# Tiles that TensorE reads moved to multiples of 512 bytes in a decoder layer

## The chip, the cores and the metric

The kernel runs on one core of one Trainium2 chip. The metric is the device time of one execution in microseconds (us); the median of three runs stands for the kernel. The engines are named as in the profile: PE is TensorE (its weight loads are listed apart as PEld), DVE is VectorE, ACT is ScalarE, POOL is GpSimd, SP is SyncE, which here issues nearly all DMAs.

## The reference

One decoder layer on 256 tokens of 2048 features in float32: two groups of 8 attention heads of 128 features each, an output projection, an MLP of 8192 hidden features with squared ReLU, and RMSNorms before, between and after.

```python
def reference(x, norm1_g, w_in, forget_b, rel_bias, outnorm_a_g, outnorm_b_g, w_out,
              norm2_g, w_mlp_in, w_mlp_out, final_norm_g):
    B, S, _ = x.shape                                   # 1, 256
    for l in range(DEPTH):                              # 1
        h = rms_norm(x, norm1_g[l])
        proj = h @ w_in[l]                              # 2048 -> 6 x 1024 + 8
        q_a, k_a, v_a, f_a, q_b, k_b, v_b = jnp.split(proj, SPLIT_POINTS, axis=-1)
        ...
        log_f = jax.nn.log_sigmoid(f_a.astype(jnp.float32) + forget_b[l].astype(jnp.float32))
        y_a = fox_attention(heads_a(q_a), heads_a(k_a), heads_a(v_a), log_f)   # causal, with a decay per key
        ...
        y_b = dilated_attention(heads_b(q_b), heads_b(k_b), heads_b(v_b), rel_bias)
        ...
        mixed = jnp.concatenate([rms_norm(y_a, outnorm_a_g[l]),
                                 rms_norm(y_b, outnorm_b_g[l])], axis=-1)
        x = x + mixed @ w_out[l]
        h = rms_norm(x, norm2_g[l])
        x = x + jnp.square(jax.nn.relu(h @ w_mlp_in[l])) @ w_mlp_out[l]
    return rms_norm(x, final_norm_g)
```

## The kernel before, in words

**Arithmetic.** Every large product is made of three: a float32 operand is split into a rounded part `hi` and the rest `lo` (both of type float32r), and hi·hi, lo·hi and hi·lo are added up in PSUM. ACT makes `hi` and DVE makes `lo`; for the weights that is `split_rows` (L168, L169), which reads the tile `raw` that a DMA has filled and writes `whi` and `wlo`.

**Chunks and steps.** The weights are cut into chunks of 512 columns: 12 chunks of q, v and k (each 16 blocks of 128 rows deep), 8 of the output projection ("o", 8 blocks), and four rounds of 4 up chunks ("u") and 4 down chunks ("d"), 16 blocks each. A step is two blocks of one chunk. The loop at the end of the kernel goes through all steps in order: it loads ahead, splits the weights up to `LEAD` = 3 steps ahead, issues the step's products, and then runs whatever was set down for that place with `at(...)` (attention, norms, drains, transposes). The order of the instructions is written out by hand, and no planner changes it.

**The products on PE.** A matmul has a stationary operand, which its own weight load (PEld) brings in first, and a moving operand, which streams through.
- q, v, k, o and d chunks (`product`, L299 to L301): stationary are 128 columns of the activations (`aT_hi`/`aT_lo` for q, v, k; `big_hi`/`big_lo` for o and d), moving are 512 columns of `whi` or `wlo`.
- u chunks (`turned_product`, L313): stationary are 128 columns of `whi` or `wlo`, moving are 256 columns of `aT_hi` or `aT_lo`.
- The last d chunk (`last_chunk`) does its second row block in two halves of 256 columns, and half of its split weights lie in `aT_hi` and `aT_lo`.
- Attention uses matmuls of 128 and 256 columns: L490 and L493 for the scores (k moving, q stationary), L538 for the values (`p_hi`/`p_lo` moving, v stationary); L520, L463 and L250 are transposes.

**Where the tiles lie.** All of SBUF's tiles come from pools (`one`, `two`, `wraw`, `wsplit`), laid out one behind the other in the order in which the pools are entered, and inside a pool in the order of first use; a tile's size is rounded up to 32 bytes. The first pool begins at byte 16512 of each partition, which is 128 past a multiple of 512. Since tiles of 8 to 2592 bytes stand among the large ones, the large ones begin at odd places. From the sizes in the code, the start of each tile modulo 512 bytes is:

| tile | role on PE | start mod 512 before |
|---|---|---|
| `xs`, `ident` | transposes | 128 |
| `aT_hi`, `aT_lo` | stationary for q, v, k; moving for u | 480 |
| `big_hi`, `big_lo` (`yT`, `hT`) | stationary for o and d | 160 |
| `whi`, `wlo` (four buffers each) | moving for q, v, k, o, d; stationary for u | 160 |
| `q_hi`, `q_lo`, `v_hi`, `v_lo` | stationary in attention | 480 |
| `k_hi`, `k_lo`, `p_hi`, `p_lo` | moving in attention | 288 |
| `gate_s`, `gate_h` | decay term of the scores | 160, 416 |
| `raw` (four buffers) | not read by PE | 160, 288, 416, 32 |

Every slice that a large product reads begins a whole number of 512 bytes behind its tile's start, so the column holds for the slices too. A float32r element has 4 bytes: a moving operand of 512 columns is 2048 bytes in a partition, one of 256 columns 1024, a stationary operand 512.

**The constant pack.** `pk` holds, for the first attention group, two triangular matrices for the decay sums, and the causal mask as three blocks of 128 columns (triangle, zeros, triangle); L503 adds the first block to the scores of the first 128 queries and the other two to those of the second.

Of the kernel before, what the change touches and what calls it, by code (L numbers as in the profile page):

```python
# [11 lines left out]
F32 = mybir.dt.float32  # L12
# [7 lines left out]
P = 128  # L20
D_MODEL = 2048
SEQ = 256
TB = SEQ // P
HD = 128
NH = 8
# [7 lines left out]
N_BUCKETS = 32  # L33
# [9 lines left out]
def _constants():  # L43
    i = np.arange(P)
    upto = (i[:, None] <= i[None, :]).astype(np.float32)
    after = (i[:, None] > i[None, :]).astype(np.float32)
    tri = np.where(i[None, :] <= i[:, None], 0.0, NEG).astype(np.float32)
    head = (i[:, None] % 32 == np.arange(NH)[None, :]).astype(np.float32)
    pack = np.concatenate([after, -upto, tri, np.zeros((P, P), np.float32), tri, head], axis=1)

    dist = np.arange(RW) - 127
    d = np.maximum(dist, 0)
    exact = N_BUCKETS // 2
    df = np.maximum(d.astype(np.float32), np.float32(1.0))
    large = exact + (
        np.log(df / np.float32(exact)) / np.float32(math.log(REL_MAX / exact)) * np.float32(N_BUCKETS - exact)
    ).astype(np.int32)
    bucket = np.where(d < exact, d, np.minimum(large, N_BUCKETS - 1))
    count = np.zeros(RW, np.int64)
    for window, dil in PATTERNS:  # L60
        count += (dist >= 0) & (dist % dil == 0) & (dist <= window)
    pick = np.zeros((N_BUCKETS + 1, RW), np.float32)
    pick[bucket, np.arange(RW)] = 1.0
    pick[N_BUCKETS] = np.where(count > 0, np.log(np.maximum(count, 1)), NEG)
    return np.ascontiguousarray(pack), pick
# [3 lines left out]
def kernel(  # L69
# [20 lines left out]
    o2d = out.rearrange("b (t p) d -> p (b t) d", p=P)  # L90
    w_in, w_out, w_up, w_down = w_in[0], w_out[0], w_mlp_in[0], w_mlp_out[0]

    one = ctx.enter_context(tc.tile_pool(name="one", bufs=1))
    two = ctx.enter_context(tc.tile_pool(name="two", bufs=2))
    wraw = ctx.enter_context(tc.tile_pool(name="wraw", bufs=4))
    wsplit = ctx.enter_context(tc.tile_pool(name="wsplit", bufs=LEAD + 1))
    psum = ctx.enter_context(tc.tile_pool(name="psum", bufs=2, space=PSUM))
    dram = ctx.enter_context(tc.tile_pool(name="dram", bufs=1, space=DRAM))
    ctx.enter_context(tc.manual_schedule())
# [74 lines left out]
    ident = one.tile([P, P], F32, name="ident")  # L174
    zeros = two.tile([P, CW], F32, name="nat")
    warm = zeros[:, :CW // 2].bitcast(BF16)
    half_t = one.tile([P, TB], F32, name="half_t")
    ones = one.tile([P, 1], F32, name="ones")
    nc.vector.memset(zeros[:, :CW // 2], 0.0)
    nc.vector.memset(half_t, -0.5)  # L180
    nc.vector.memset(ones, 1.0)
# [12 lines left out]
    for c in range(1, 4):  # L194
        load_x(4 * c, 4 * c + 4)
        load(2 * c)
    fb = one.tile([P, NH], F32, name="fb")
    relx = one.tile([N_BUCKETS + 1, NH], F32, name="relx")
    nc.vector.memset(relx, 1.0)
    pk = one.tile([P, 5 * P + NH], F32, name="pk")  # L200
    pick_sb = two.tile([P, RW], F32, name="pr")[:N_BUCKETS + 1]

    def small_loads():
# [4 lines left out]
        nc.sync.dma_start(pk, pack)  # L208
        nc.sync.dma_start(pick_sb, pick)

    mcat = pk[:, 2 * P:5 * P]
    head = pk[:, 5 * P:]
    gcat = one.tile([P, TB, P], F32R, name="gcat")


# [4 lines left out]
            nc.tensor.matmul(pw, warm[:, :P], warm, start=True, stop=True)  # L220

    nc.scalar.activation(ones, ones, AF.Copy)
    gT = one.tile([P, 48], F32, name="gT")

    def gains(k0, k1):
        p = psum.tile([P, 512], F32, name="tr")
# [28 lines left out]
    def rsqrt(dst, ssq, n):  # L255

        w = dst.shape[1]
        v = two.tile([P, TB], F32, name="rs_v")[:, :w]
        t = two.tile([P, TB], F32, name="rs_t")[:, :w]
        nc.vector.tensor_scalar(v, ssq, 1.0 / n, EPS, op0=ALU.mult, op1=ALU.add)  # L260
        nc.gpsimd.tensor_tensor(dst, v, half_t[:, :w], op=ALU.pow)
        nc.vector.tensor_tensor(t, dst, dst, op=ALU.mult)
        nc.vector.tensor_tensor(t, t, v, op=ALU.mult)
        nc.vector.tensor_scalar(t, t, -0.5, 1.5, op0=ALU.mult, op1=ALU.add)
        nc.vector.tensor_tensor(dst, dst, t, op=ALU.mult)

    ssq1 = one.tile([P, TB, 4], F32, name="ssq1")
    ssq1s = one.tile([P, TB], F32, name="ssq1s")
    rstd1 = one.tile([P, TB], F32, name="rstd1")
    rstdq = one.tile([P, TB], F32, name="rstdq")  # L270

    def first_squares(t, c):
        unused = yT_hi[:, 2 * (4 * t + c):2 * (4 * t + c) + 2, :].rearrange("p k s -> p (k s)")
# [66 lines left out]
        side.setdefault(i, []).append((f, a))  # L340


    logf = one.tile([P, TB, NH], F32, name="logf")
    lf_hi, lf_lo = (
        two.tile([P, 3 * P], F32R, name=n)[:, :2 * P].rearrange("p (t q h) -> p t q h", t=TB, q=4)
        for n in ("p_hi", "p_lo")
# [10 lines left out]
    def forget_gates():  # L357
        f = psum.tile([P, 512], F32, name="tr")
        for t in range(TB):
            nc.tensor.transpose(f[:, 2 * t * NH:2 * (t + 1) * NH], fTs[0][:, t * P:(t + 1) * P], ident[:2 * NH, :2 * NH])  # L360
        z = one.tile([P, TB, NH], F32, name="fz")
        e = one.tile([P, TB, NH], F32, name="fe")
        u = one.tile([P, TB, NH], F32, name="fu")
        d = one.tile([P, TB, NH], F32, name="fd")
        n = one.tile([P, TB, NH], F32, name="fn")
        for t in range(TB):
            for k, add in enumerate((fb, z[:, t, :])):
                nc.vector.scalar_tensor_tensor(
                    z[:, t, :], f[:, (2 * t + k) * NH:(2 * t + k + 1) * NH], rstd1[:, t:t + 1], add,
                    op0=ALU.mult, op1=ALU.add,  # L370
                )
        nc.scalar.activation(e, z, AF.Abs)
        nc.scalar.activation(e, e, AF.Exp, scale=-1.0)

        nc.vector.tensor_scalar(u, e, 1.0, None, op0=ALU.add)
        nc.vector.tensor_scalar(d, u, 1.0, None, op0=ALU.subtract)
        nc.vector.tensor_scalar(n, d, 0.0, None, op0=ALU.is_equal)
        nc.vector.tensor_tensor(d, d, n, op=ALU.add)
        nc.vector.reciprocal(d, d)
        nc.scalar.activation(u, u, AF.Ln)  # L380
        nc.vector.tensor_tensor(u, u, d, op=ALU.mult)
        nc.vector.tensor_tensor(u, u, n, op=ALU.add)
        nc.vector.tensor_tensor(u, u, e, op=ALU.mult)
        nc.vector.scalar_tensor_tensor(logf, z, 0.0, u, op0=ALU.min, op1=ALU.subtract)
        split_psum(lf_hi[..., :NH], lf_lo[..., :NH], logf[:, :, None, :].to_broadcast([P, TB, 4, NH]))
# [25 lines left out]
    relT = one.tile([P, NH, SEQ], F32, name="relT")  # L411
# [67 lines left out]
    def scores(g, h):  # L479

        half, kind = groups[g][3:]
        hd = half * 4 + h
# [14 lines left out]
        decay.pop(hd, None)  # L497
        neg = two.tile([P, 3 * P], F32, name="neg")
        pr = two.tile([P, 3 * P], F32, name="pr")
        st = two.tile([P, 3, TB], F32, name="st")  # L500
        for t, c0, c1 in spans:
            add = mcat[:, c0:c1] if kind == 0 else relT[:, hd, SEQ - (c1 - c0):]
            nc.vector.tensor_tensor_reduce(  # L503
                neg[:, c0:c1], s[:, c0:c1], add, -1.0, BIG, ALU.add, ALU.min, st[:, 0, t:t + 1]
            )
# [41 lines left out]
        split_psum(yT_hi[:, hd, :], yT_lo[:, hd, :], y[:, :SEQ], gT[:, 32 + hd:33 + hd])  # L547
        seen[kind] += 1

    rstdo = [one.tile([P, TB], F32, name=f"rstdo{k}") for k in range(2)]  # L550

    def group_norm(kind):
        p = psum.tile([P, 512], F32, name="tr")
# [2 lines left out]
                             skip_group_check=True)  # L556
        rsqrt(rstdo[kind], p[:, :TB], D_GRP)

    ssq2 = one.tile([P, TB, 4], F32, name="ssq2")
    ssq2s = one.tile([P, TB], F32, name="ssq2s")  # L560
    rstd2 = one.tile([P, TB], F32, name="rstd2")
    rstd2sq = one.tile([P, TB], F32, name="rstd2sq")

    def drain_o(kind, c, ci):
        acc = accs.pop(ci)
# [26 lines left out]
            )  # L592

    gf = relT.rearrange("p h s -> p (h s)")
    ssq3 = one.tile([P, TB, 5], F32, name="ssq3")
    ssq3s = one.tile([P, TB], F32, name="ssq3s")
    rstd3 = one.tile([P, TB], F32, name="rstd3")

    def load_gf():
        nc.sync.dma_start(  # L600
# [21 lines left out]
    def put_gain(t, cs):  # L622
        nc.vector.tensor_tensor(xs[:, t, cs], xs[:, t, cs], gf[:, cs], op=ALU.mult)
# [5 lines left out]

    def finish(t, n, cs):  # L630
        r, s = rstd3[:, t:t + 1], ssq3s[:, t:t + 1]
        v = two.tile([P, 1], F32, name="fi_v")
        u = two.tile([P, 1], F32, name="fi_u")
        ru = two.tile([P, 1], F32, name="fi_ru")
        nc.vector.tensor_scalar(v, ssq3[:, t, n:n + 1], s, 1.0 / D_MODEL, op0=ALU.add, op1=ALU.mult)
        nc.gpsimd.tensor_tensor(r, v, half_t[:, :1], op=ALU.pow)
        put_gain(t, cs)
        nc.vector.scalar_tensor_tensor(u, r, v, r, op0=ALU.mult, op1=ALU.mult)
        nc.vector.tensor_scalar(u, u, -0.5, 1.5, op0=ALU.mult, op1=ALU.add)
        nc.gpsimd.tensor_tensor(ru, r, u, op=ALU.mult)  # L640
        for c, (a, b) in enumerate(((0, 384), (384, 896), (896, 1408), (1408, 2048))):
            xc = xs[:, t, a:b]
            if c == 1:
                nc.scalar.activation(xc, xc, AF.Copy, scale=ru)
            else:
                nc.vector.tensor_scalar(xc, xc, r, u, op0=ALU.mult, op1=ALU.mult)  # L646
            nc.sync.dma_start(o2d[:, t, a:b], xc)
# [27 lines left out]
    for ci, (what, key, *_rest) in enumerate(chunks[:-1]):  # L675
        e = last_slot[what, key]
# [9 lines left out]
        elif what in "qk":  # L686
# [4 lines left out]
            if what == "k":  # L691
                kind = groups[key][4]
                for h in range(4):
                    n = e + 6 + 4 * h
# [45 lines left out]
    upto = {final - 4: final, final - 3: final + 1, final - 2: final + 3, final - 1: final + 5}  # L740
# [42 lines left out]
```

## Time and profile before

| | |
|---|---|
| median of three runs | 1136.5 us (1136.19 to 1137.27) |
| time of the profiled execution | 1136.86 us |
| its span in the profile | 1135.1 us |
| PE busy | 1124.0 us, 99% |
| PEld, DVE, ACT, POOL busy | 87%, 56%, 46%, 3% |
| DMA | 209.15 MB, mean 184 GB/s |
| mean granted PE clock | 0.998 |

Matmuls overlap in the profile: one that starts is listed with its whole way through the array, so the durations in the rows are longer than the distance between two starts. What the engine needs for one of a long row of matmuls is the distance from start to start, and it is read here as a stretch of time divided by the number of matmuls that start in it.

### The profile page before, as it was taken

The numbers are of one execution on the slowest core, as the hardware profiler recorded it, in microseconds if no ns is written. First come the engines' busy times: TensorE is split into PE (matmuls) and PEld (weight loads), VectorE is DVE, ScalarE is ACT, GpSimd is POOL, SyncE is SP. The second block draws the span as 40 slices with busy tenths as digits, with TensorE's granted clock in tenths as the row PEclk, the third lists the DMA queues.
The fourth block names the chain that finished last, engine by engine and source line by source line (L and its number), as shares of the span: only waits on it lengthen the run. The fifth ranks groups of instructions, "written<-read, shape, count | busy, mean of one in ns | idle before, by whom it ended". The sixth has DMA issues, their size and how long they took to land.

```text
span 1135.1 us, 16038 instructions
## 1 busy us (share of the span) xinstructions
PE 1124.0 (99%) x6635; PEld 988.8 (87%) x6635; DVE 639.7 (56%) x795; ACT 521.9 (46%) x675; POOL 31.7 (3%) x57
## 2 busy tenths in 40 slices
PE   9999999999999999999999999999999999999996
PEld 6778888888888889998889998889998889999886
DVE  5665656556566665555555555545555554555564
ACT  5545545545445554454334444343544433454451
POOL 0100200100001000000000000000000000000000
PEclk9999999999999999999999999999999999999999
DMA  8655454454545556556555655566465566556642
GB/s 312 224 183 183 154 185 149 149 185 149 186 156 178 155 179 192 187 179 212 196 185 164 208 186 188 200 199 192 152 220 187 186 193 192 187 171 206 240 148 74
DMA packets 104933, 209.15 MB, mean 184 GB/s; under 512 B 3651, under 2 KB 4508, under 8 KB 104732
## 3 DMA queue, kind: packets, MB, share of 16 engines
q1 hardware_dynamic: 104556, 207.06, 55.8%
q0 software_dynamic: 304, 1.06, 0.3%
q8 instruction: 52, 0.85, 0.3%
q14 instruction: 21, 0.17, 0.0%
HBM read 206.00 MB, written 2.11 MB: 183 GB/s over the span
## 4 chain that ended last, share of the span: by engine, by line
PE 98%; DMA 1%; DVE 0%; SPq 0%; ACT 0%; POOL 0%; issue 0%; DVEq 0%
PE acc L313 32%; PE acc L299 21%; PE acc L301 21%; PE acc L300 21%; PE sc L493 1%; PE sc L538 1%; PE tr L463 1%; DMA raw<-in_w_in_dram 1%; PE tr L250 1%; PE tr L520 0%; PE sc L333 0%; PE sc L490 0%; DVE wlo L169 0%; ACT whi L168 0%; DVE xs L646 0%; SPq L185 0%
## 5 line engine op out<-in xcount | busy, mean ns | idle before, releaser
L169 DVE TENSOR_TENSOR wlo<-raw,whi 128x1024 fp32r<-128x1024 f32 (+1 forms) x381 | 464.1, 1224 | 374.4 <-ACT whi L168 371.6
L168 ACT ACTIVATE whi<-raw 128x1024 fp32r<-128x1024 f32 (+1 forms) x381 | 399.8, 1055 | 404.2 <-PE acc L300 241.4
L313 PE MATMUL acc<-aT_hi,whi 128*128 128x256 f32 x1024 | 287.2, 280 | 0.0
L313 PE MATMUL acc<-aT_hi,wlo 128*128 128x256 f32 x1024 | 286.1, 279 | 0.0
L313 PE MATMUL acc<-aT_lo,whi 128*128 128x256 f32 x1024 | 286.0, 279 | 0.0
L299 PE MATMUL acc<-whi,big_hi 128*128 128x512 f32 (+1 forms) x632 | 246.0, 389 | 0.0
L301 PE MATMUL acc<-wlo,big_hi 128*128 128x512 f32 (+1 forms) x632 | 244.7, 387 | 0.0
L300 PE MATMUL acc<-whi,big_lo 128*128 128x512 f32 (+1 forms) x632 | 244.5, 387 | 0.0
L313 PEld LDWEIGHTS acc<-aT_hi,wlo 128*128 128x128 f32 x1024 | 192.8, 188 | 0.0
L313 PEld LDWEIGHTS acc<-aT_hi,whi 128*128 128x128 f32 x1024 | 192.3, 188 | 0.2
L313 PEld LDWEIGHTS acc<-aT_lo,whi 128*128 128x128 f32 x1024 | 191.6, 187 | 0.2
L299 PE MATMUL acc<-whi,aT_hi 128*128 128x512 f32 x384 | 157.0, 409 | 0.0
L300 PE MATMUL acc<-whi,aT_lo 128*128 128x512 f32 x384 | 152.5, 397 | 0.0
L301 PE MATMUL acc<-wlo,aT_hi 128*128 128x512 f32 x384 | 152.3, 397 | 0.0
L301 PEld LDWEIGHTS acc<-wlo,big_hi 128*128 128x128 f32 x632 | 118.7, 188 | 24.4
L300 PEld LDWEIGHTS acc<-whi,big_lo 128*128 128x128 f32 x632 | 118.8, 188 | 23.4
L299 PEld LDWEIGHTS acc<-whi,big_hi 128*128 128x128 f32 x632 | 118.8, 188 | 22.9
L301 PEld LDWEIGHTS acc<-wlo,aT_hi 128*128 128x128 f32 x384 | 72.5, 189 | 17.4
L299 PEld LDWEIGHTS acc<-whi,aT_hi 128*128 128x128 f32 x384 | 72.7, 189 | 15.3 <-issue 0.6
L300 PEld LDWEIGHTS acc<-whi,aT_lo 128*128 128x128 f32 x384 | 72.7, 189 | 14.0 <-DVE aT_lo L240 0.2
L237 DVE TENSOR_TENSOR big_lo<-nat,big_hi 128x512 fp32r<-128x512 f32 x32 | 22.2, 693 | 22.3 <-ACT big_hi L236 22.3
L507 ACT ACTIVATE pr<-neg,st 128x128 f32<-128x128 f32 (+1 forms) x32 | 14.3, 448 | 40.8 <-DVE st L503 40.8
(160 smaller groups left out, 533.7 us busy)
## 6 DMA issues: line engine op xcount, KB each, us to landing
raw<-in_w_mlp_in_dram SPq DMA_DIRECT2D x64, 1024.0 KB, 5.3
raw<-in_w_mlp_out_dram SPq DMA_DIRECT2D x64, 1024.0 KB, 5.2
raw<-in_w_in_dram SPq DMA_DIRECT2D x42, 1024.0 KB, 5.2
raw<-in_w_out_dram SPq DMA_DIRECT2D x16, 1024.0 KB, 5.1
raw<-in_w_in_dram SPq DMA_DIRECT2D x4, 1040.0 KB, 5.3
raw<-in_w_in_dram SPq DMA_DIRECT2D x3, 512.0 KB, 8.6
xs<-in_x_dram SPq DMA_DIRECT2D x3, 512.0 KB, 9.6
big_lo<-rel_d POOLq DMA_DIRECT2D x1, 1024.0 KB, 7.3
```

What stands on the lines that cost most here:

```text
L168: nc.scalar.activation(hi, t, AF.Copy)
L169: nc.vector.tensor_tensor(lo, t, hi.bitcast(F32), op=ALU.subtract)
L237: nc.vector.tensor_tensor(lo, src, hi.bitcast(F32), op=ALU.subtract)
L250: nc.tensor.transpose(p[:, j * SEQ + t * P:j * SEQ + (t + 1) * P], xs[:, t, c:c + P], ident)
L299: nc.tensor.matmul(acc, xh, hi[:, j, cols], start=go, stop=False)
L300: nc.tensor.matmul(acc, xl, hi[:, j, cols], start=False, stop=False)
L301: nc.tensor.matmul(acc, xh, lo[:, j, cols], start=False, stop=end)
L313: nc.tensor.matmul(acc, w[:, j, b * P:(b + 1) * P], a[:, kt, :], start=kt == 0 and b % 2 == 0 and n == 0, stop=kt == kts - 1 and n == 2, s ...
L463: nc.tensor.transpose(p[:, j * SEQ + t * P:j * SEQ + (t + 1) * P], ts[t][:, h * P:(h + 1) * P], ident)
L493: nc.tensor.matmul(s[:, c0:c1], q[:, h, t * P:(t + 1) * P], k[:, h, :c1 - c0], start=n == 0 and kind == 1, stop=n == 2,)
L507: nc.scalar.activation(pr[:, c0:c1], neg[:, c0:c1], AF.Exp, bias=st[:, 0, t:t + 1], scale=-1.0, accum_out=st[:, 1, t:t + 1],)
L538: nc.tensor.matmul(y[:, o0:SEQ], v[:, t, h * P:(h + 1) * P], p[:, c0:c1], start=t == 0 and n == 0, stop=t == 1 and n == 2,)
```

## The change

All small tiles (up to the 2080 bytes of `pk`) move to a new pool, `few`, which is entered last and so lies behind everything else. A new pool in front, `lead_in`, holds `gT` alone, stretched from 48 to 96 columns (384 bytes), so that `one` begins at byte 16896, 33 times 512. What is left in `one`, `two`, `wraw` and `wsplit` has sizes that are multiples of 512 bytes, but for `raw` (8320 bytes, four buffers, together 65 times 512) and `wf` (128 bytes, four buffers, the last of `wsplit`). By the sizes, then, `xs`, `ident`, `aT`, `big`, `whi`, `wlo`, q, k, v, `p`, `nat`, `gate_s`, `gate_t`, `gate_h` and `gcat` all begin at 0 modulo 512 afterwards, and `raw` at 0, 128, 256 and 384.

The mask loses its first block: both row blocks now read the end of the pair (zeros, triangle), the first its last 128 columns, the second all 256. `pk` shrinks from 2592 to 2080 bytes a partition. No instruction is added, removed or moved, and no loop or buffer count changes.

```diff
-    pack = np.concatenate([after, -upto, tri, np.zeros((P, P), np.float32), tri, head], axis=1)
+    pack = np.concatenate([after, -upto, np.zeros((P, P), np.float32), tri, head], axis=1)
...
+    lead_in = ctx.enter_context(tc.tile_pool(name="lead_in", bufs=1))
     one = ctx.enter_context(tc.tile_pool(name="one", bufs=1))
     two = ctx.enter_context(tc.tile_pool(name="two", bufs=2))
     wraw = ctx.enter_context(tc.tile_pool(name="wraw", bufs=4))
     wsplit = ctx.enter_context(tc.tile_pool(name="wsplit", bufs=LEAD + 1))
+    few = ctx.enter_context(tc.tile_pool(name="few", bufs=1))
...
-    half_t = one.tile([P, TB], F32, name="half_t")
-    ones = one.tile([P, 1], F32, name="ones")
+    half_t = few.tile([P, TB], F32, name="half_t")
+    ones = few.tile([P, 1], F32, name="ones")
...
-    pk = one.tile([P, 5 * P + NH], F32, name="pk")
+    pk = few.tile([P, 4 * P + NH], F32, name="pk")
...
-    mcat = pk[:, 2 * P:5 * P]
-    head = pk[:, 5 * P:]
+    mask = pk[:, 2 * P:4 * P]
+    head = pk[:, 4 * P:]
...
-    gT = one.tile([P, 48], F32, name="gT")
+    gT = lead_in.tile([P, 96], F32, name="gT")[:, :48]
...
-        v = two.tile([P, TB], F32, name="rs_v")[:, :w]
+        v = few.tile([P, TB], F32, name="rs_v", bufs=2)[:, :w]
...
-        st = two.tile([P, 3, TB], F32, name="st")
+        st = few.tile([P, 3, TB], F32, name="st", bufs=2)
         for t, c0, c1 in spans:
-            add = mcat[:, c0:c1] if kind == 0 else relT[:, hd, SEQ - (c1 - c0):]
+            add = (mask if kind == 0 else relT[:, hd])[:, SEQ - (c1 - c0):]
...
```

The lines left out move `fb`, `relx`, `rs_t`, `ssq1`, `ssq1s`, `rstd1`, `rstdq`, `logf`, `fz`, `fe`, `fu`, `fd`, `fn`, `rstdo0`, `rstdo1`, `ssq2`, `ssq2s`, `rstd2`, `rstd2sq`, `ssq3`, `ssq3s`, `rstd3`, `fi_v`, `fi_u` and `fi_ru` to `few` in the same way, with the buffer counts they had.

More of the change, by code (lines that the diff above doesn't have):

```diff
@@ L196 @@
         load(2 * c)
-    fb = one.tile([P, NH], F32, name="fb")
-    relx = one.tile([N_BUCKETS + 1, NH], F32, name="relx")
+    fb = few.tile([P, NH], F32, name="fb")
+    relx = few.tile([N_BUCKETS + 1, NH], F32, name="relx")
     nc.vector.memset(relx, 1.0)
-    pk = one.tile([P, 5 * P + NH], F32, name="pk")
+    pk = few.tile([P, 4 * P + NH], F32, name="pk")
     pick_sb = two.tile([P, RW], F32, name="pr")[:N_BUCKETS + 1]
@@ L257, in rsqrt @@
         w = dst.shape[1]
-        v = two.tile([P, TB], F32, name="rs_v")[:, :w]
-        t = two.tile([P, TB], F32, name="rs_t")[:, :w]
+        v = few.tile([P, TB], F32, name="rs_v", bufs=2)[:, :w]
+        t = few.tile([P, TB], F32, name="rs_t", bufs=2)[:, :w]
         nc.vector.tensor_scalar(v, ssq, 1.0 / n, EPS, op0=ALU.mult, op1=ALU.add)
@@ L265, in rsqrt @@
         nc.vector.tensor_tensor(dst, dst, t, op=ALU.mult)
[L267 to L270, printed above, removed]
+    ssq1 = few.tile([P, TB, 4], F32, name="ssq1")
+    ssq1s = few.tile([P, TB], F32, name="ssq1s")
+    rstd1 = few.tile([P, TB], F32, name="rstd1")
+    rstdq = few.tile([P, TB], F32, name="rstdq")
     def first_squares(t, c):
@@ L340, in at @@
         side.setdefault(i, []).append((f, a))
-    logf = one.tile([P, TB, NH], F32, name="logf")
+    logf = few.tile([P, TB, NH], F32, name="logf")
     lf_hi, lf_lo = (
@@ L360, in forget_gates @@
             nc.tensor.transpose(f[:, 2 * t * NH:2 * (t + 1) * NH], fTs[0][:, t * P:(t + 1) * P], ident[:2 * NH, :2 * NH])
[L361 to L365, printed above, removed]
+        z = few.tile([P, TB, NH], F32, name="fz")
+        e = few.tile([P, TB, NH], F32, name="fe")
+        u = few.tile([P, TB, NH], F32, name="fu")
+        d = few.tile([P, TB, NH], F32, name="fd")
+        n = few.tile([P, TB, NH], F32, name="fn")
         for t in range(TB):
@@ L548, in values @@
         seen[kind] += 1
-    rstdo = [one.tile([P, TB], F32, name=f"rstdo{k}") for k in range(2)]
+    rstdo = [few.tile([P, TB], F32, name=f"rstdo{k}") for k in range(2)]
     def group_norm(kind):
@@ L557, in group_norm @@
         rsqrt(rstdo[kind], p[:, :TB], D_GRP)
[L559 to L562, printed above, removed]
+    ssq2 = few.tile([P, TB, 4], F32, name="ssq2")
+    ssq2s = few.tile([P, TB], F32, name="ssq2s")
+    rstd2 = few.tile([P, TB], F32, name="rstd2")
+    rstd2sq = few.tile([P, TB], F32, name="rstd2sq")
     def drain_o(kind, c, ci):
@@ L594 @@
     gf = relT.rearrange("p h s -> p (h s)")
-    ssq3 = one.tile([P, TB, 5], F32, name="ssq3")
-    ssq3s = one.tile([P, TB], F32, name="ssq3s")
-    rstd3 = one.tile([P, TB], F32, name="rstd3")
+    ssq3 = few.tile([P, TB, 5], F32, name="ssq3")
+    ssq3s = few.tile([P, TB], F32, name="ssq3s")
+    rstd3 = few.tile([P, TB], F32, name="rstd3")
     def load_gf():
@@ L631, in finish @@
         r, s = rstd3[:, t:t + 1], ssq3s[:, t:t + 1]
-        v = two.tile([P, 1], F32, name="fi_v")
-        u = two.tile([P, 1], F32, name="fi_u")
-        ru = two.tile([P, 1], F32, name="fi_ru")
+        v = few.tile([P, 1], F32, name="fi_v", bufs=2)
+        u = few.tile([P, 1], F32, name="fi_u", bufs=2)
+        ru = few.tile([P, 1], F32, name="fi_ru", bufs=2)
         nc.vector.tensor_scalar(v, ssq3[:, t, n:n + 1], s, 1.0 / D_MODEL, op0=ALU.add, op1=ALU.mult)
```

## The prediction

> **What bounds the kernel now.** I read the page first: busy times, the granted clock, the chain that ended last.
>
> ```profile
> span 1135.1 us, 16038 instructions
> PE 1124.0 (99%) x6635; PEld 988.8 (87%) x6635; DVE 639.7 (56%) x795; ACT 521.9 (46%) x675; POOL 31.7 (3%) x57
> PEclk9999999999999999999999999999999999999999
> PE 98%; DMA 1%; DVE 0%; SPq 0%; ACT 0%; POOL 0%; issue 0%; DVEq 0%
> ```
>
> PE is the path from end to end, at full clock in every slice, so only two things can move the time: fewer matmuls, or less time from one matmul to the next. The waits of PE confirm that nothing else holds it:
>
> ```profile
> PE sc L220 <- DVE relx L199: 1.2, 1, 1.2
> PE tr L250 <- DVE aT_lo L240: 0.8, 1, 0.8
> PE tr L227 <- DMA grow<-in_norm_g_dram: 0.5, 1, 0.5
> ```
>
> Three waits, 2.5 us in all. The change keeps every instruction, so the question is the distance between matmul starts, and whether that distance hangs on where operands lie. The groups by form give the counts:
>
> ```profile
> L313 PE MATMUL acc<-aT_hi,whi 128*128 128x256 f32 x1024 | 287.2, 280 | 0.0
> ...
> L299 PE MATMUL acc<-whi,big_hi 128*128 128x512 f32 x616 | 241.5, 392 | 0.0
> ...
> L299 PE MATMUL acc<-whi,aT_hi 128*128 128x512 f32 x384 | 157.0, 409 | 0.0
> ```
>
> With the hi·hi, lo·hi and hi·lo terms that is 3072 matmuls of the u chunks, 1848 of o and d, 1152 of q, v and k. Next, long stretches of one kind: the chain's pieces in order of time for u, windows for the others.
>
> ```profile
> 593.22 90.45 PE acc L313 x768
> ...
> 770.75 90.45 PE acc L313 x768
> ```
>
> ```profile
> 136.96:166.13 29.17, 29.17 (x126) 1.00 0.56 181
> ...
> 505.97:593.05 87.08, 87.08 (x386) 1.00 0.59 192
> ```
>
> A u matmul (256 columns) takes 90.45 / 768 = 117.8 ns. In the first window 125 q, v, k matmuls start and one is still running from before: 29.17 / 125 = 233.4 ns. The second window is one round of d: 384 start in it (two u matmuls reach in from before): 87.08 / 384 = 226.8 ns.
>
> This pair is the first finding. Both kinds stream the same tiles, `whi` and `wlo`, 512 columns, at the same granted clock (1.00) and nearly the same DMA share; the stationary operand begins at 480 modulo 512 in the one and at 160 in the other. The distance differs by 6.6 ns, 3%. The end of the kernel gives two more pairs, in starts of the first and the last of a row:
>
> ```profile
> 1103.89 0.40 PE L299 MATMUL acc<-aT_hi,big_hi 128*128 128x512 f32 x1
> ...
> 1109.40 0.40 PE L299 MATMUL acc<-whi,big_hi 128*128 128x512 f32 x1
> ...
> 1119.89 0.28 PE L299 MATMUL acc<-whi,big_hi 128*128 128x256 f32 x1
> ...
> 1120.61 0.28 PE L299 MATMUL acc<-aT_hi,big_hi 128*128 128x256 f32 x1
> ```
>
> Between 1103.89 and 1109.40 the 512 columns come from `aT` (480) against the same stationary tile as d: 24 matmuls, 229.6 ns each. Between 1119.89 and 1120.61 six matmuls of 256 columns come from `whi` (160): 120 ns each. So the start of either operand changes the cadence by up to 3%.
>
> **How much of a matmul isn't streaming.** At equal starts (160 and 160), 512 columns take 226.8 ns and 256 take 120: 106.8 ns for 256 columns, 0.417 ns a column, are streaming, and 13.2 ns a matmul are not. The rest is then 19.8 ns for q, v, k (233.4 - 213.6) and 11.0 for u (117.8 - 106.8). The short matmuls of attention show how it grows:
>
> ```profile
> 267.81 0.28 PE L538 MATMUL sc<-p_hi,v_hi 128*128 128x256 f32 x1
> ...
> 268.15 0.22 PE L538 MATMUL sc<-p_hi,v_hi 128*128 128x128 f32 x1
> 268.20 0.28 PE L538 MATMUL sc<-p_lo,v_hi 128*128 128x128 f32 x1
> ...
> 268.43 0.45 PE L299 MATMUL acc<-whi,aT_hi 128*128 128x512 f32 x1
> ```
>
> Three of 256 columns in 0.34 us: 113 ns, 7 over streaming. One of 128 in 0.05 to 0.06 us, against 53 of streaming. The next two, of 128 columns, take 0.23 us, 115 ns each: twice the streaming, so there the weight load sets the pace, and 115 ns is the nearest row for what one costs.
>
> **A rule that fits most rows.** Cut the partition into blocks of 512 bytes and count the blocks that a moving operand touches: 5 for 512 columns from 160 (88 + 128 + 128 + 128 + 40 columns), 3 for 256, 2 for 128 from 288. At 2.64 ns a block, 5 give 13.2 (d), 3 give 7.9 (measured 7), 2 give 5.3 (a few). u has 3.1 ns more than its 3 blocks; its first piece is only 8 columns long. q, v, k have 6.6 more, with the stationary operand cut after 8 columns. Not explained is the 120 at the end (5.3 more than its 3 blocks), which matters below.
>
> **The change part by part.**
> *o and d, 1848 matmuls.* From 0 the moving operand touches 4 blocks: -2.64 ns each, -4.9 us. No row shows 512 columns faster than d, so the price is bounded: at best all 13.2 ns go (-24.4 us); at worst d falls into the state of q, v, k, 233.4 (+12.2 us). I take the block rule, because four kinds of row agree on it.
> *q, v, k, about 1000 of 1152.* The windows of the opening leave the others out, since there inputs still set the pace:
>
> ```profile
> 0.00:20.00 20.00, 17.50 (x66) 11.70 (x67) 9.28 (x19) 10.44 (x18) 1.19 (x8) 1.00 0.90 311
> 20.00:40.00 20.00, 20.00 (x97) 15.88 (x96) 16.29 (x32) 13.98 (x25) 3.60 (x11) 1.00 0.84 291
> ```
>
> (163 matmuls of all kinds in 40 us.) Of the remaining, each goes from 233.4 to what d then has, 224.2: -9.2 us. Bounds: 213.6 (-19.8 us) and no gain (0).
> *u, 3072 matmuls.* Two blocks give 112.1, but the weight load stands beside it at 115 by the attention rows, and I take that: -2.8 ns, -8.6 us. Bounds: 106.8 (-33.8 us) and the 120 of equal starts (+6.8 us).
> *Attention, transposes, norms.* Unchanged in number. By the code L493 and L538 issue 192 matmuls for the 16 heads; a block less each is 0.5 us, taken as nothing.
> *Splits and drains.* Their tiles move too. In one u round:
>
> ```profile
> L169 DVE TENSOR_TENSOR wlo<-raw,whi 128x1024 fp32r<-128x1024 f32 x32 | 39.0, 1225 | 36.2 <-ACT whi L168 35.9
> ...
> L168 ACT ACTIVATE whi<-raw 128x1024 fp32r<-128x1024 f32 x32 | 33.6, 1057 | 41.7 <-PE acc L313 40.1 <-PE acc L300 1.7
> ```
>
> A step has 24 u matmuls, 2.83 us, against 1.23 us of DVE; PE covers them, and a step shortened by 3% still does. Should an address cost DVE or ACT something, it would have to double the split before PE waits. DMA stands at a share of 0.59 in the window above and rises to 0.60 in a stretch 2% shorter.
> *Mask and pack.* The same 16 instructions read one pair of blocks; 64 KB fewer come in.
>
> ```profile
> L503 DVE CUSTOM_DVE_ANT_0 neg<-sc,pk x16: 290/356/421, 97.1 to 194.8; 128x128 f32<-128x128 f32 x8, 128x256 f32<-128x256 f32 x8
> L208 SPq DMA_DIRECT2D pk<-in_pack_dram x1: 352/352/352, 22.1 to 22.1; - x1
> ...
> DMA to landing us min/median/max: 6.7/6.7/6.7
> ```
>
> Issued at 22.1, landed by 29, first read at 97.1 by the mask: nothing. Pools add no wait, since each tile keeps its buffers.
>
> **Sum.** -4.9 - 9.2 - 8.6 = -22.7 us. The profiled execution took 1136.86 us (span 1135.1, 1.8 outside), 0.03% over the median: 1136.9 - 22.7 = 1114.2, or 1114 against the median. A difference under 0.2% (2.3 us) can't be told from none.
>
> **Row against rule.** After a disturbance, products of o begin slow and speed up:
>
> ```profile
> 332.13 0.40 PE L299 MATMUL acc<-whi,big_hi 128*128 128x512 f32 x1
> ...
> 332.83 0.39 PE L299 MATMUL acc<-whi,big_hi 128*128 128x512 f32 x1
> ...
> 333.99 0.39 PE L301 MATMUL acc<-wlo,big_hi 128*128 128x512 f32 x1
> ...
> 334.90 0.49 PE L520 MATMUL tr<-ident,pr 128*128 128x128 f32 x3
> ```
>
> Three matmuls in 0.70 us, 233 ns; the last four of this row 0.91, 228. Same operands' starts, two cadences: weight load and stream disturb each other until they have slipped out of step. The Trainium skill (TensorE: Matmul & The Clock Gate, "Step-by-step: what each phase is for") says the opposite: two independent read ports, so that loading the next weights takes no bandwidth from the running matmul. By that rule the stationary start would matter to nothing, and q, v, k would gain only the block of o and d (-2.6 us instead of -9.2; sum -16). The trace disagrees with it, 233.4 against 226.8. The same page ("Wait — 56ns, not 53.3ns?") gives the distance as N / 2.4 GHz plus 2.5 ns; the streaming agrees (0.417 ns a column), the 13.2 ns do not.
>
> **The rivals.**
> 1. *Everything that isn't streaming comes from the starts.* o and d -24.4, q, v, k -19.8, u held by the weight load at -8.6: -52.8, 1084. For it: 13 ns is much for five boundaries. Against it: no start in any row brings 256 columns under 7 ns of rest, and a read from 0 still passes block ends. By the skill's 2.5 ns it would be 1136.5 - 19.8 - 17.3 - 8.6 = 1091.
> 2. *Only the stationary start counts:* q, v, k fall to d's 226.8 (-6.6), nothing else moves: 1130.
> 3. *Only the relation counts.* Afterwards all starts are equal, like today's 160 and 160. Then 512 columns take 226.8 and 256 take 120: q, v, k -6.6, u +6.8: 1137, no change. The end of the kernel shows just these two rows, which speaks for it.
> 4. *Slower: in step for good.* Load and stream begin at the same place of a block in every matmul and never slip apart, as q, v, k never do today. u goes to 120 (+6.8), o and d to 233.4 (+12.2), q, v, k stay: 1143 with u alone, 1155 with both. It decides once o and d stay above 226.8 while u is above 117.8. Against it: today's equal starts do slip apart.
> That the change doesn't reach the chip isn't one: the starts follow from the sizes.
>
> **How the numbers follow.** Forecast 0.42 (its own range 1104 to 1126, u between 112 and 117.8); rival 1 0.12; rival 2 0.15; rival 3 0.14; rival 4 0.17. Faster is the forecast with rivals 1 and 2, 0.69; same rival 3, 0.14; slower rival 4, 0.17. The range runs from rival 1 (1084) to rival 4 with u alone (1143), leaving out what lies beyond each, some 0.15.
>
> **What would show it.** A round of u at 768 x 115 = 88.3 us instead of 90.45; a round of d at 384 x 224.2 = 86.1 instead of 87.08; q, v, k at 224 in their window, and no slow start after attention. u at 92 us would be rivals 3 or 4, and d tells which (87 or 89.6). DVE and ACT means should stay at 1225 and 1057 ns. Wrong as a whole would be a d round outside 82 to 89.6 us.

## The result and the profile after

The changed kernel takes 1138.34 us (median of 20 runs, 1137.6 to 1141.1) against 1136.63 us for the kernel before (20 runs, 1135.89 to 1137.46): ratio 1.0016, 95% interval 1.0009 to 1.0023. It is slower by 0.16%, less than the 0.2% that the prediction set as no difference. 1114 was forecast. The small sum hides two larger terms of opposite sign. (The ratios in this document are taken over all runs and can differ by a few units of the last digit from the quotient of the medians.)

Four lines of the changed kernel's page:

```profile
span 1136.3 us, 16038 instructions
...
PE 1124.0 (99%) x6635; PEld 993.6 (87%) x6635; DVE 639.5 (56%) x795; ACT 522.0 (46%) x675; POOL 32.2 (3%) x57
...
PEclk9999999999999999999999999999999999999999
...
PE 98%; DMA 1%; DVE 0%; SPq 0%; ACT 0%; POOL 0%; issue 0%; DVEq 0%
```

Same instructions, same clock, PE still the path. The lines of the code have moved by three: L316 is the old L313, L302 to L304 the old L299 to L301. Below are the long pieces of the chain for u (start, us, matmuls), then windows over q, v, k and over one round of d (length, PE busy, matmuls, clock, DMA share, GB/s):

```profile
414.58 87.84 PE acc L316 x732
...
589.49 92.15 PE acc L316 x768
...
768.71 92.15 PE acc L316 x768
...
947.92 92.15 PE acc L316 x768
```

```profile
134.84:163.20 28.36, 28.36 (x126) 1.00 0.57 186
502.25:589.33 87.08, 87.08 (x387) 1.00 0.59 192
```

- u: 92.15 / 768 = 120.0 ns instead of 117.8. A round costs 1.70 us more, the four together 6.7 us. Added up from start to start over all 3072 matmuls, the trace before has 362.0 us and the one after 368.8.
- q, v, k: 125 matmuls start in the first window, 28.36 / 125 = 226.9 ns instead of 233.4. Added up from start to start over all 1152 of them, the sums are 275.7 and 270.6 us: -5.1 us.
- d: 384 matmuls in 87.08 us, 226.8 ns, unchanged to the hundredth. Over all 1848 of o and d the sums are 421.1 and 421.0 us.

(The cadence of a row of matmuls is here the distance from one start to the next.) These are the two cadences that the old kernel had where both operands began at 160: 120 ns for 256 columns and 226.8 ns for 512. After the change both operands of every large product begin at the same place, and the long stretches above have those two cadences.

The durations on the other engines did not move. The DVE and ACT groups of the changed kernel in one round of u:

```profile
L172 DVE TENSOR_TENSOR wlo<-raw,whi 128x1024 fp32r<-128x1024 f32 x32 | 38.9, 1225 | 37.8 <-ACT whi L171 37.6
```

```profile
L171 ACT ACTIVATE whi<-raw 128x1024 fp32r<-128x1024 f32 x32 | 33.5, 1056 | 43.3 <-PE acc L316 41.6 <-PE acc L303 1.7
```

1225 and 1056 ns a split are what they were before (1225, 1057), although all their tiles begin elsewhere.

### The profile page after: what moved, and what is told of

It reads as the page before. It is cut to its first block, busy times and chain, and to the rows that moved or that the text cites. A ratio compares the mean times of both kernels' runs of the same rounds, so it can differ in the third digit from the quotient of the medians.

```text
span 1136.3 us, 16038 instructions
## 1 busy us (share of the span) xinstructions
PE 1124.0 (99%) x6635; PEld 993.6 (87%) x6635; DVE 639.5 (56%) x795; ACT 522.0 (46%) x675; POOL 32.2 (3%) x57
## 4 chain that ended last, share of the span: by engine, by line
PE 98%; DMA 1%; DVE 0%; SPq 0%; ACT 0%; POOL 0%; issue 0%; DVEq 0%
PE acc L316 32%; PE acc L302 21%; PE acc L304 20%; PE acc L303 20%; PE sc L496 1%; PE sc L541 1%; PE tr L466 1%; DMA raw<-in_w_in_dram 1%; PE tr L253 1%; PE tr L523 0%; PE sc L336 0%; PE sc L493 0%; DVE wlo L172 0%; ACT whi L171 0%; DVE xs L649 0%; SPq L188 0%
## 5 line engine op out<-in xcount | busy, mean ns | idle before, releaser
L316 PE MATMUL acc<-aT_hi,whi 128*128 128x256 f32 x1024 | 289.9, 283 | 0.0
L316 PE MATMUL acc<-aT_hi,wlo 128*128 128x256 f32 x1024 | 289.8, 283 | 0.0
L316 PE MATMUL acc<-aT_lo,whi 128*128 128x256 f32 x1024 | 289.8, 283 | 0.0
L302 PE MATMUL acc<-whi,big_hi 128*128 128x512 f32 (+1 forms) x632 | 245.7, 389 | 0.0
L304 PE MATMUL acc<-wlo,big_hi 128*128 128x512 f32 (+1 forms) x632 | 244.4, 387 | 0.0
L316 PEld LDWEIGHTS acc<-aT_lo,whi 128*128 128x128 f32 x1024 | 196.6, 192 | 0.2
L316 PEld LDWEIGHTS acc<-aT_hi,whi 128*128 128x128 f32 x1024 | 196.6, 192 | 0.2
L316 PEld LDWEIGHTS acc<-aT_hi,wlo 128*128 128x128 f32 x1024 | 196.6, 192 | 0.0
L302 PE MATMUL acc<-whi,aT_hi 128*128 128x512 f32 x384 | 154.6, 403 | 0.0
L304 PE MATMUL acc<-wlo,aT_hi 128*128 128x512 f32 x384 | 150.2, 391 | 0.0
L303 PE MATMUL acc<-whi,aT_lo 128*128 128x512 f32 x384 | 150.1, 391 | 0.0
L304 PEld LDWEIGHTS acc<-wlo,big_hi 128*128 128x128 f32 x632 | 118.7, 188 | 24.2
L302 PEld LDWEIGHTS acc<-whi,big_hi 128*128 128x128 f32 x632 | 118.8, 188 | 23.3
L304 PEld LDWEIGHTS acc<-wlo,aT_hi 128*128 128x128 f32 x384 | 72.1, 188 | 15.7
L302 PEld LDWEIGHTS acc<-whi,aT_hi 128*128 128x128 f32 x384 | 72.2, 188 | 13.8 <-ACT fu L383 0.6
```

Of the source, the lines that this page charges most:

```text
L302: nc.tensor.matmul(acc, xh, hi[:, j, cols], start=go, stop=False)
L303: nc.tensor.matmul(acc, xl, hi[:, j, cols], start=False, stop=False)
L304: nc.tensor.matmul(acc, xh, lo[:, j, cols], start=False, stop=end)
L316: nc.tensor.matmul(acc, w[:, j, b * P:(b + 1) * P], a[:, kt, :], start=kt == 0 and b % 2 == 0 and n == 0, stop=kt == kts - 1 and n == 2, s ...
```

## The experiments

Two theories stood against each other: B, the prediction's blocks of 512 bytes, in which a start at 0 is best; and R, in which only the distance from the start of the stationary to the start of the moving operand counts. Distances below are in bytes.

**map: cadence by starts.** A kernel of nothing but matmul series on two tiles that begin at a multiple of 512. A series has n moving columns, its moving operand begins at m and its stationary operand of c columns at s, and REP is 60:

```python
for k, (n, m, s, c) in enumerate(series()):
    ...
    acc = psum.tile([P, 512], F32, name=name, tag="acc")
    for i in range(REP):
        m0 = (i % 3) * 512 + m // 4
        s0 = (i % 6) * 128 + s // 4
        nc.tensor.matmul(acc[:c, :n], st[:, s0:s0 + c], mv[:, m0:m0 + n], start=i == 0, stop=i == REP - 1)
```

> This kernel leaves out the whole layer: it loads x, copies it into two float32r tiles that both begin at a multiple of 512 bytes, writes x out, and then runs 56 series of 60 matmuls each, with a weight load each, on nothing but PE. A series has one number of columns (512 or 256) and one pair of starts inside the two tiles; the distance between matmul starts is read for each series. Theory R (only the distance modulo 512 from the start of the stationary to the start of the moving operand counts): pairs with the same distance agree within 1 ns wherever both begin; distance 0 gives 226.8 ns at 512 columns and 120.0 at 256; distance 192 gives 233.4 at 512; distance 320 gives 229.6 at 512 and 117.8 at 256; somewhere between there is a distance that is better than 0. Theory B (the prediction's blocks of 512 bytes): starts at 0 and 0 are the best of all, about 224 at 512 and 112 to 115 at 256; a moving start of 160 costs 2.6 ns more, one of 480 about 5.5 more, whatever the other operand. With a stationary operand of 16 columns, R gives one value for all starts; B gives 2.6 ns more for every start but 0.

Eight of the map's PE rows for 512 columns in order of time, one row for each series (start, length, name); from one start to the next is 60 matmuls:

```profile
25.89 13.76 PE L59 MATMUL saa<-mv,st 128*128 128x512 f32 x60
39.49 14.17 PE L59 MATMUL sab<-mv,st 128*128 128x512 f32 x60
53.49 13.91 PE L59 MATMUL sac<-mv,st 128*128 128x512 f32 x60
67.23 14.17 PE L59 MATMUL sad<-mv,st 128*128 128x512 f32 x60
...
137.30 13.79 PE L59 MATMUL sai<-mv,st 128*128 128x512 f32 x60
150.92 14.17 PE L59 MATMUL saj<-mv,st 128*128 128x512 f32 x60
...
248.72 13.76 PE L59 MATMUL saq<-mv,st 128*128 128x512 f32 x60
262.32 14.16 PE L59 MATMUL sar<-mv,st 128*128 128x512 f32 x60
```

Distance 0 (saa): 13.60 us, 226.7 ns. Distance 32 (sab): 14.00 us, 233.3. Distance 64 (sac): 13.74, 229.0. Distance 256 (sai): 13.62, 227.0 with its slow start, so the pattern has a period of 256, not 512. Series saq has both operands at 160 and runs as saa does. A series often begins slow before it settles, so the steady value is the mean of its last 30 intervals. At 512 columns the steady values of all eight pairs outside the first sweep agree within 0.1 ns with the pair of the same distance in it. That is R, and B is out: starts at 0 and 0 are no better than 160 and 160.

R missed three points. At 512 columns no distance was better than 0. At 256 columns, distance 192 came out at 113.3 ns in two series and 117.8 in three. And with a stationary operand of only 16 columns the moving start still mattered: 226.7 to 231.7 ns at 512 columns, 113.3 to 116.7 at 256. A short weight load disturbs too, at other distances. Two of its rows, 512 columns at distance 32 and 256 at distance 0:

```profile
373.01 13.78 PE L59 MATMUL saz<-mv,st 128*16 128x512 f32 x60
...
584.47 6.97 PE L59 MATMUL sca<-mv,st 128*16 128x256 f32 x60
```

Their steady values, 226.7 and 113.3 ns, are the lowest of the map, and the lowest with 128 stationary columns are the same. So the length of the weight load does not set these two values.

**at320: the distance put back, the alignment kept.**

```diff
+    one.tile([P, 80], F32, name="gap_a")
     aT_hi = one.tile([P, KT, SEQ], F32R, name="aT_hi")
     aT_lo = one.tile([P, KT, SEQ], F32R, name="aT_lo")
+    one.tile([P, 48], F32, name="gap_b")
```

> The changed kernel with an empty tile of 320 bytes ahead of the two tiles of activations (aT) and one of 192 bytes behind them: aT begins at 320 modulo 512, and every other tile that TensorE reads in bulk stays at 0. Theory R (only the distance of the two starts modulo 512 counts): aT then stands to the split weights as it did before the change (480 to 160), so both effects of the change go back: q, v, k from 227.0 to 233.3 ns a matmul, u from 120.0 to 117.8, o and d stay at 226.7; the time is that of the kernel before, ratio 0.999 to 1.001. Theory B (blocks of 512 bytes): u reads 3 blocks instead of 2 and q, v, k load a cut stationary operand, so nothing gets faster than in the changed kernel: u at 120 or more, ratio 1.0016 or more against the kernel before.

1136.49 us against 1136.47 for the kernel before, ratio 0.9996 (0.9986 to 1.0005). The chain's u pieces of this kernel:

```profile
592.50 90.45 PE acc L318 x768
...
770.04 90.45 PE acc L318 x768
```

Back at 90.45 us a round, with q, v, k at 233.3 ns and d at 226.8. Both effects of the change hang on the distance between `aT` and the split weights. The rest of it (the pool `few`, the shorter mask, the other starts) is worth nothing that these runs can tell from zero.

**map256: all pairs at 256 columns.** 64 pairs of starts in steps of 32 and 14 finer ones, each series behind the same six matmuls of 512 columns.

> Again nothing of the layer but x in and out; series of 60 matmuls of 256 columns with a weight load each, all 64 pairs of starts of the moving and the stationary operand in steps of 32 bytes modulo 256, and 14 finer starts of the moving one. Ahead of each series stand the same six matmuls of 512 columns from 0 and 0, so that every series begins from the same state. In the first map the pairs at distance 192 modulo 256 split: 113.3 ns in two series, 117.8 in three. Theory H (the distance modulo 256 alone decides, and the split was left by the series before): all eight pairs of one distance now agree within 0.5 ns, and distance 192 gives 113.3 throughout. Theory A (each operand's own start modulo 256 counts besides): only pairs with the stationary operand at 0 give 113.3 at distance 192, others stay at 117.8. Nothing should be under 113.3, which is 0.4427 ns a column, the same as 226.67 ns for 512 columns. If the conflict is between single accesses of 32 bytes or wider, finer starts give the value of a neighbour in steps of 32; if it depends on bytes, they give values between.

Steady cadence by distance, from the last 30 intervals of each series (both maps for 512 columns, map256 for 256):

| distance modulo 256 | 512 columns, ns | 256 columns, ns (of eight pairs) |
|---|---|---|
| 0 | 226.7 | 120.0 |
| 32 | 233.4 | 116.7 (once 117.8) |
| 64 | 228.9 | 117.8 six times, 113.3 twice |
| 96 | 233.3 | 120.0 |
| 128 | 233.3 | 118.7 (once 120.0) |
| 160 | 234.3 | 117.3 six times, 118.7 twice |
| 192 | 233.3 | 113.3 five times, 117.8 three times |
| 224 | 233.3 | 118.3 |

The PE rows of four series (60 matmuls and the tail of the last, 0.28 us): stationary and moving start 0 and 0, 0 and 192, 64 and 0, 0 and 112.

```profile
27.57 7.36 PE L56 MATMUL saa<-mv,st 128*128 128x256 f32 x60
...
78.65 7.23 PE L56 MATMUL sag<-mv,st 128*128 128x256 f32 x60
...
163.46 6.98 PE L56 MATMUL saq<-mv,st 128*128 128x256 f32 x60
...
612.30 7.00 PE L56 MATMUL scr<-mv,st 128*128 128x256 f32 x60
```

(7.36 - 0.28) / 59 = 120.0 ns, then 117.8, 113.6 and 113.9 with their slow starts. Sag and saq have the same distance, 192 modulo 256, and differ. Theory H in its strict form (one value for each distance) and theory A (only a stationary start of 0 gives 113.3) both fell: saq has its stationary operand at 64, sag at 0. What holds is that a distance has one or two steady states. (Distance 32 is another: 117.8 in both series of the first map, 116.7 in all but one here.) Nothing lies below 113.3, as expected. Finer starts count too, since a distance of 8 gave 126.7 ns and 112 gave 113.3, while both neighbours of 112 in steps of 32 (96 and 128) are slow.

**u64 and u192: the distance of u alone.** q, v, k keep the changed kernel's distance of 0, and u gets its own view, 64 or 192 bytes further in the same tiles, which are 256 bytes longer for it. This is u192; u64 has `64 // 4` for `192 // 4`:

```diff
-    aT_hi = one.tile([P, KT, SEQ], F32R, name="aT_hi")
-    aT_lo = one.tile([P, KT, SEQ], F32R, name="aT_lo")
+    U_AT = 192 // 4
+    aTs = [one.tile([P, KT * SEQ + 64], F32R, name=n) for n in ("aT_hi", "aT_lo")]
+    aT_hi, aT_lo = (a[:, :KT * SEQ].rearrange("p (k s) -> p k s", k=KT) for a in aTs)
+    uT_hi, uT_lo = (a[:, U_AT:U_AT + KT * SEQ].rearrange("p (k s) -> p k s", k=KT) for a in aTs)
...
-        terms = ((hi, aT_hi), (hi, aT_lo), (lo, aT_hi))
+        terms = ((hi, uT_hi), (hi, uT_lo), (lo, uT_hi))
```

(`to_features` writes the second norm's output through the same view.)

> The same, but with the activations of the u chunks 64 bytes further instead of 192. That gives u the distance it had before the change (320, which is 64 modulo 256), and leaves q, v, k, o and d as the change has them: the gain of q, v, k alone. Theory R: u back from 120.0 to 117.8 ns, q, v, k at 227.0: before less 1000 x 6.3 ns less the share of the rest, 1131.5, ratio 0.9955. Theory B: u no faster than in the changed kernel, ratio 1.0016 or more. A theory in which only multiples of 512 bytes count (64 and 192 alike are not): u64 and u192 give the same time.

> The changed kernel, in which the second half (u chunks) writes and reads its activations 192 bytes further in the same two tiles, which are 256 bytes longer for it: u then has a distance of 192 from the stationary weights (at 0) to the moving activations, while q, v, k, o and d keep a distance of 0. Theory R with the first map (192 and 0 gave 113.3 ns): u falls from 120.0 to 113.3 ns, 3072 x 6.67 = 20.5 us; q, v, k stay at 227.0 and o and d at 226.7; 1138.3 - 20.5 = 1118, ratio to the kernel before 0.984. If u falls into the other state seen at this distance (117.8 ns): 1131.5, ratio 0.9955. Theory B (blocks of 512 bytes): u reads 3 blocks instead of 2 and gets no faster: ratio 1.0016 or more.

u64: 1131.69 us, ratio 0.9952 (0.9939 to 0.9964), as R said: the gain of q, v, k without u's loss (u is back at 90.45 us a round). u192: 1128.45 us, ratio 0.9922 (0.9908 to 0.9935), between the two values expected. The chain's u pieces of u192 show why:

```profile
409.83 2.83 PE acc L319 x24
...
414.91 82.99 PE acc L319 x732
...
584.95 90.45 PE acc L319 x768
...
762.45 90.45 PE acc L319 x768
```

82.99 / 732 = 113.4 ns in the first round, 117.8 in the later ones, with the same addresses. The first 24 matmuls of the first round still took 2.83 / 24 = 117.9 ns; then come four transposes for the second norm. 732 x 4.4 ns = 3.2 us is what u192 gains over u64 (1131.69 - 1128.45).

**kick: what brings a round into the fast state.** u192 with some extra matmuls on PE in the second to fourth round.

```diff
+    KICKS = {(1, 0): (1, "turn"), (1, 2): (2, "turn"), (2, 0): (3, "turn"), (2, 2): (4, "turn"),
+             (3, 0): (1, "short"), (3, 2): (2, "short")}
...
+            if key in KICKS:
+                at(e - 15, kick, *KICKS[key])
```

> The kernel u192 with a few extra matmuls on PE, whose results nothing reads, in the second to fourth round of u, 12 matmuls after the first chunk begins and again 12 after the third begins: one, two, three and four transposes of 128 columns, then one and two float32r matmuls of 128 columns. In u192 the first round of u ran at 113.3 ns and the three later ones at 117.8, with the same addresses; the first one has four transposes for the second norm ahead of its long stretch, the later ones come straight from d. Theory H (at distance 192 two steady states exist, and the way in decides): at least the four transposes bring u from 117.8 to 113.3 ns until the round ends, 512 or fewer matmuls x 4.4 ns; some of the other kicks may as well, and the fourth round shows whether a short matmul does. Theory T (something else in the later rounds, such as d's drains or the loads, holds them at 117.8): every stretch stays at 117.8 and the time is that of u192 plus the extra matmuls, 1129.5.

1124.19 us in one run. Three of the kicks, and then the chain's u pieces of this kernel, cut where a kick stands:

```profile
585.42 0.27 PE L347 MATMUL tr<-ident 128*128 128x128 f32 x1
...
630.76 0.38 PE L347 MATMUL tr<-ident 128*128 128x128 f32 x2
...
761.64 0.49 PE L347 MATMUL tr<-ident 128*128 128x128 f32 x3
```

```profile
585.69 45.23 PE acc L319 x384
...
631.14 42.19 PE acc L319 x372
...
762.13 43.55 PE acc L319 x384
...
806.11 42.19 PE acc L319 x372
...
936.83 45.28 PE acc L319 x384
...
982.28 43.87 PE acc L319 x372
```

One transpose: 45.23 / 384 = 117.8 ns. Two: 42.19 / 372 = 113.4, until the round ends. Three: 113.4. The four came when the round was already fast, and it stayed so. One and two short float32r matmuls: 117.9, no effect. Each kick was tried once. So the two states exist at the same addresses in the same loop, and what comes before decides between them. Theory T is out.

**u112: a distance that came out fast after a slow start.** The edit is that of u192 with `112 // 4`.

> The kernel u192 with 112 bytes instead of 192 between the start of the stationary and of the moving operand of u. In the second map this distance, tried once and with the stationary operand at 0, came to 113.3 ns after ten matmuls. Theory H with one steady state at 112: all four rounds of u at 113.3 ns, 3072 x 4.4 ns less than u64, 1118. If 112 has two states like 192: some rounds at 113.3, the others higher, 1119 to 1132. Theory that only multiples of 32 bytes matter: u as at a distance of 96, 120.0 ns, 1138.

1119.89 us in one run, then timed as u112t:

> The kernel u112 timed against the kernel before. Theory R (the distance of the two starts modulo 256 sets the cadence; 112 has one steady state): 1119.9, ratio 0.9852 with an interval clear of 1, all rounds of u at 113.3 ns again. If the state were chance, some execution or some round would show 117.8 and the times would scatter by up to 13 us.

1118.31 us (1118.01 to 1119.49), ratio 0.9841 (0.9827 to 0.9854). The chain's u pieces of u112t:

```profile
414.90 83.01 PE acc L319 x732
...
584.98 87.08 PE acc L319 x768
...
759.13 87.08 PE acc L319 x768
...
933.28 87.08 PE acc L319 x768
```

All four rounds at 87.08 / 768 = 113.4 ns.

**odd112: the same distances in the large products, without the aligned starts.** The kernel before, with the view of u112 and an empty tile of 64 bytes behind the two tiles of `aT`, which puts `aT`, `big` and the split weights at 224 modulo 256:

```diff
+    one.tile([P, 16], F32, name="gap")
```

> The kernel before, without any of the change's pools, with an empty tile of 64 bytes behind aT and with u's activations 112 bytes further in tiles that are 256 bytes longer. No tile that TensorE reads in bulk begins at a multiple of 512: aT, big and the split weights all begin at 224 modulo 256, so q, v, k, o and d have a distance of 0 and u one of 112. Theory R: the same cadences as u112t (227.0, 226.7, 113.3 ns) and the same time within 1 us, 1120; starting at a multiple of 512 is worth nothing by itself. A theory in which the aligned start is worth something besides the distance: slower than u112t, by 2.6 ns a matmul under the block rule, 3072 + 3000 matmuls, 16 us, 1136.

1117.8 us (1117.58 to 1118.28), ratio 0.9835 (0.9822 to 0.9849). Its first and last long u pieces:

```profile
584.54 87.08 PE acc L317 x768
...
932.83 87.08 PE acc L317 x768
```

No tile of `aT`, `big` or the split weights is at a multiple of 512, and the kernel is as fast as u112t. Multiples of 512 are worth nothing here; 64 bytes in one place and a shift of 112 in another take 19 us off the kernel before.

## Why the prediction was wrong

*What bounds the kernel: right.* PE is the path and the distance between matmul starts is the time: each of these kernels moved by its cadences and by little else.

*That starts matter: right,* and so was the reading of 233.4 against 226.8 on one moving tile. But what matters is where one operand begins relative to the other, not where each begins.

*"106.8 ns for 256 columns, 0.417 ns a column, are streaming": wrong, and the first step that failed.* It was the difference between 226.8 (512 columns) and 120 (256 columns), both at distance 0. But distance 0 is the best for 512 columns and not for 256: the 120 is 6.7 ns above the lowest value at 256 columns, and the 226.8 is the lowest at 512. The lowest values of the maps are 226.67 and 113.33, which is 0.4427 ns a column at both sizes and leaves nothing over. So d had no 13.2 ns to give and was already at the best value that any run showed; the term for o and d (-4.9 us forecast) measured 0.

*The block rule: wrong.* It was fitted to that false remainder. Rows agreed on it because at 0.4427 ns a column even the lowest cadence shows, against 0.417, a rest that grows with its columns (13.2 and 6.6 ns at 512 and 256), as a count of blocks does. The row that the prediction called not explained, the 120 at the end, was the one to follow.

*q, v, k (-9.2 us forecast): right sign, size off.* They fell to d's cadence, 6.5 ns, not to 224.2; the 2.64 ns of the block were not there. And fewer of them came to that cadence than the 1000 assumed: in the changed kernel's trace 679 of the 1152 intervals are 224 to 227 ns (7 before the change), and 413 are 228 to 239. The slow starts that the prediction expected to go did not all go. u64, which has this gain alone, is 5.2 us under the kernel before in its comparison.

*u (-8.6 us forecast): wrong sign,* +6.7 us. The prediction took 115 ns from the attention rows over the 120 of the row with equal starts; that row's bound, +6.8, was the value that came. A round of u at 92 us beside one of d at 87 was the prediction's own sign for rival 3, and it came: rival 3 named this mechanism, both terms and 1137, and had a chance of 0.14.

*The weight load at 115 ns as a floor for u: wrong.* u112t runs at 113.4 with a weight load for each matmul.

*Splits, mask, pack, pools at nothing: right,* shown by at320.

*Row against rule: the row was right.* The Trainium skill (TensorE: Matmul & The Clock Gate, "Step-by-step: what each phase is for") has the next weight load take nothing from the running matmul. At the same clock, the same matmuls took 113.3 to 126.7 ns where nothing but the starts of the two operands was changed (map256), so in these runs the two do get in each other's way. By the Trainium skill's N / 2.4 GHz plus 2.5 ns (the same page, "Wait — 56ns, not 53.3ns?") 512 columns would take an estimated 215.8 ns; no series or long stretch of float32r matmuls of 512 columns here has a steady cadence below 226.7.

**What stays open.** The runs show that distance sets the cadence, with a period of 256 bytes, and that some distances have two steady states. They do not show where in the memory or in PE the two reads meet, why two transposes changed the state and one did not, or whether transposes help at other distances: at 64, where two of eight series came out at 113.3 ns, the kernel before, at320 and u64 stayed at 117.8 in all four rounds, the one behind four transposes included. Nor do they show whether 112 always comes out fast or is the best of all fine distances: only 14 were tried.

## What to carry to other kernels

When PE is busy all the time, divide a long stretch by its matmuls, kind by kind, and compare kinds that differ in one operand's place: the 3% difference found here belonged to a pair of tiles and not to one tile. Put two operands at a chosen distance, by a small gap or a shifted view, and measure; do not expect a round address to help, and look for a distance that comes out fast in every round, since one with two states can lose half of its gain to how the stretch was entered. When one row contradicts a rule that fits the others, work out what the change does by that row before putting a chance on the rule.

## What the runs showed of the hardware

- The lowest steady cadence of float32r matmuls in these runs is 0.4427 ns a moving column at a granted clock of 1.00: 226.67 ns for 512 columns, 113.33 for 256, one weight load of 128 columns each included. With weight loads of 16 columns it is the same.
- The distance between the starts of the stationary and the moving operand, modulo 256 bytes, adds 0 to 7.6 ns to a matmul of 512 columns (in steps of 32) and 0 to 13.3 to one of 256 (126.7 at a distance of 8). At a distance of 0 the starts themselves made no difference: 0 and 0 and 160 and 160 ran alike at both sizes, and so did 224 and 224 at 256.
- The best distance depends on the columns: 0 is best for 512 (226.7), and for 256 (120.0) no distance in steps of 32 is slower.
- Some distances have two steady states: 113.3 or 117.8 ns at 192, each held for hundreds of matmuls. Two transposes on PE moved a running loop from the slow to the fast one, in one run.
- VectorE and ScalarE splits of 128 x 1024 took 1225 and 1056 or 1057 ns in a round of u, before and after the change, with their tiles at other starts.
